# Hybrid decoder trunk on one core: ScalarE evacuation of latents, token-major reciprocals, earlier weight splits and piecewise recurrence units in the first stage

## The chip, the cores and the metric

The kernel runs on one core of a Trainium2 chip. Five engines work side by side, each through its own instructions in order: PE (TensorE, matmul; its weight loads are shown as PEld), DVE (VectorE), ACT (ScalarE), POOL (GpSimd) and SP (SyncE, whose queue issues the DMAs of this stage). The metric is the device time of one execution in microseconds. Each kernel is run several times and the median is compared.

## The reference

Input `x` has 2048 tokens of 1024 numbers. What the first stage computes is the first norm and everything per token that hangs on the input projection; the rest is named in a line each.

```python
h = rmsnorm(x, mix_norm_g)
cols = h @ w_in                      # 35 column chunks of 128 and less: recurrence, gates, q, kv, kr
# recurrence, per head of 64: z = z_in + (prev - z_in) * mu; r, k, v, decay, a, g out of z, then
#   state = state * w + sa * (kk * a) + v * k        over the tokens
# latents, q_d of 384 and kv_d of 256 columns:
q  = rmsnorm(q_d, g_qa) @ w_q_up
kv = rmsnorm(kv_d, g_kva) @ w_kv_up
gate = sigmoid(cols of the gates)
# later stages: causal attention, the scan over chunks, merge and output projection,
# hierarchical mixture of experts, final norm
```

A norm is `y * rsqrt(mean(y*y) + eps) * g`. Here the norm of `x` is not applied to `h` before the projection but to the projected columns, so each chunk is multiplied by the reciprocal root `xrs` of its tokens when it leaves PSUM.

## The kernel before

`phase_a` is the first stage, 0 to 1062 us of the profile. It takes two halves of 1024 tokens, each as `n` = 0, 1 of 512 tokens, with channels on the partitions and tokens along the free side. For each of the 35 chunks of a half (order `worder`: 0 and 1 inputs of the loras, 2 to 13 recurrence, five gates 14 to 18, KV 33 and 34, Q 30 to 32, gate 19, `kr`, the other gates) and each `n`, `a_mm` issues 24 matmuls of 128x512 (three products of a hi/lo split, L151 to L153 in `mm3`) into a PSUM tile of tag `am`, of which there are four. All other small matmuls go through four tiles of tag `rw`.

Weights come by DMA to `awr`; `a_split` (L424) makes hi and lo `aw0`, `aw1` with ScalarE and VectorE or GpSimd, two buffers each, one chunk ahead. A recurrence chunk is evacuated by `a_lerp` (L451: `zin` on VectorE, `zmu` on ScalarE, `z` on VectorE). When three chunks (r, k, v) of a head pair stand, `rw_unit` (L463) prepares the scan: it yields nine times and so has ten pieces. Its names: `kraw`, `ta`, `f`, `bk`, `ar`, `u` are [128 x 512] operands; `aa` are masked products (matmuls L551, evacuation L554); L567 a sum over heads, whose result goes to `bon`; `lora("g")` follows; then three times four transposes (L590) of `hat`, `hat` and `z` go to `rw`, ScalarE copies each to `tok` (L592), and four DMAs from it go to `BKd` (twice) or `Vd`. All of its tiles have one buffer except `hat`; a copy to `tok` waits for the DMAs of the last one. There are eight units in each half, p = 0 to 3 of n = 0, 1. For p < 3 the unit is issued whole, right behind its third chunk; for p = 3 it goes on the list `gens`, and `bg(k)` runs k pieces of that list in between other work, here beside the gates.

KV and Q chunks are latents: `mla_evac` (L253) multiplies by `xrs` on VectorE into `zc` (L259) and squares on ScalarE into `zacc`. `mla_norm` (L273) sums these squares over partitions with a matmul of ones (`sums`, L210), takes root (ScalarE) and reciprocal (VectorE) of the whole [128 x 512] tile and scales. `x_rms` (L228) does the same for `x`. `invert` (L777) is an inversion of small triangular matrices on VectorE (L799, L801), 62 steps that start when the units of a half are stored: it loads `inv` and `si` by DMA, L784 and L792 scale them; then it goes on beside the chunks of KV, Q and gates.

What a function issues is set in order for each engine by a list scheduler when the kernel is built, out of modelled costs; on the chip each engine then goes through its own row in that order. The order of the rows after the edit is therefore shown below, and not only the diff.

Of the kernel before, what the change touches and what calls it, by code (L numbers as in the profile page):

```python
# [10 lines left out]
F32 = mybir.dt.float32  # L11
F32R = mybir.dt.float32r
# [3 lines left out]
AF = mybir.ActivationFunctionType  # L16
OP = mybir.AluOpType
# [4 lines left out]
S, D = 2048, 1024  # L22
# [24 lines left out]
CST = {}  # L47
CFIRST = 128

# [38 lines left out]
class K:  # L88
# [67 lines left out]
    def rope_tables(self, pool):  # L156

        nc = self.nc
        sh = [128, 256]
        self.ropeT = self.dram("ropeT", [2, 8, 16, S])  # L160
        pi = pool.tile(sh, I32, name="posi")
        self.dma(pi, self.I["pos"])
        a, n, z, s, c, u = (pool.tile(sh, F32, name="rt_" + k) for k in "anzscu")
        nc.gpsimd.tensor_copy(u, pi)
# [44 lines left out]

    def sums(self, acc, n, scale):  # L210

        nc = self.nc
        ps = self.pst("rw", 4)
        nc.tensor.matmul(ps, self.c["ones"], acc, start=True, stop=True)
        nc.scalar.activation(n, ps, AF.Sqrt, scale=scale, bias=self.eps[:, 0:1])
        nc.vector.reciprocal(n, n)

# [9 lines left out]

    def x_rms(self, n):  # L228
        self.rs[n] = self.ap.tile([128, 512], F32, name="xrs%d" % n)
        self.sums(self.xacc[n], self.rs[n], 1.0 / D)  # L230

# [21 lines left out]
    def mla_evac(self, pool, ps, key, n, j):  # L253
        nc = self.nc
        if j == 0:
            self.zc[key, n] = (pool.tile([128, 3, 512], F32, name="zc", bufs=2),
                               pool.tile([128, 512], F32, name="zacc", bufs=2))
        zc, acc = self.zc[key, n]
        nc.vector.tensor_tensor(out=zc[:, j], in0=ps, in1=self.rs[n], op=OP.mult)  # L259
        sq = pool.tile([128, 512], F32, name="zsq") if j else acc  # L260
        nc.scalar.activation(sq, zc[:, j], AF.Square)
        if j:
            nc.vector.tensor_tensor(out=acc, in0=acc, in1=sq, op=OP.add)
# [9 lines left out]
    def mla_norm(self, pool, key, n):  # L273
        nc = self.nc
        zc, acc = self.zc.pop((key, n))
        nk, g0, dim = (3, 50, 384) if key == "q" else (2, 53, 256)
        yield "w"
        yield "w"
        rt = pool.tile([128, 512], F32, name="zrs")
        self.sums(acc, rt, 1.0 / dim)  # L280
        cT = [pool.tile([128, 3, 512], F32R, name="cT%d" % j, bufs=2) for j in range(2)]
# [142 lines left out]
    def a_split(self):  # L424
        rv = self.wraw.pop(0)
        hl = [self.ap.tile([128, 8, 128], F32R, name="aw%d" % j, bufs=2) for j in range(2)]
        if rv.shape[2] == 64:
# [7 lines left out]
    def a_mm(self, ci, n, last):  # L435
        while len(self.live) < 2 and self.wraw:
            self.a_split()
# [25 lines left out]
    def rw_unit(self, pool, p, q, zr, zk, zv, x1, xg):  # L463
# [117 lines left out]
        for j, src in enumerate(("b", "k", "v")):  # L581
# [7 lines left out]
            for i in range(4):  # L589
                nc.tensor.transpose(ps[:, i * 128:(i + 1) * 128], x[:, i * 128:(i + 1) * 128], self.ident)  # L590
            tk = t("tok")
            A.activation(tk, ps, AF.Copy)  # L592
# [7 lines left out]
    def phase_a(self):  # L600
# [3 lines left out]
        with ExitStack() as st:  # L604
# [6 lines left out]
            self.wpos = self.wsplit = 0  # L611
            self.wraw, self.live, self.ht, self.zc, self.rs, self.cT, self.xacc = [], [], [[None] * 8, [None] * 8], {}, {}, {}, {}
            gens = []
# [46 lines left out]
            xs = [self.x_load(xp, 0, 0, True)]  # L660
            self.dma(self.c["ones"], self.I["cst"][:, :CFIRST])
            xs.append(self.x_load(xp, 0, 1))
# [6 lines left out]
            for half in range(2):  # L669
                with pool("rw%d" % half) as rp:  # L670
# [26 lines left out]
                    for ci in range(2, 14):  # L697
                        for n in range(2):
# [3 lines left out]
                            if e == 2:  # L702
                                g = self.rw_unit(rp, p, 2 * half + n, z[n, 0], z[n, 1], z[n, 2], x1[n], xg[n])
                                if p == 3:
                                    gens.append(g)
                                else:
                                    for _ in g:
                                        pass
                    for ci in G[:5]:
# [1102 lines left out]
```

## Time and profile before

| | us |
|---|---|
| median of 3 runs | 2710.06 (2707.57 to 2715.52) |
| profiled execution | 2706.18 |
| its span on the core | 2704.4 |
| first stage of it | 0 to 1062 |
| PE busy in the span | 2493.0 (92%) |
| VectorE busy | 1957.0 (72%) |
| ScalarE busy | 1424.3 (53%) |
| GpSimd busy | 961.8 (36%) |

The span is what the profiler saw on the core. The times in all rows below are microseconds from its start. Engines are busy beside one another; a share of busy time says nothing by itself about which of them sets the end.

### The profile page before, as it was taken

The numbers are of one execution on the slowest core, as the hardware profiler recorded it, in microseconds if no ns is written. First come the engines' busy times: TensorE is split into PE (matmuls) and PEld (weight loads), VectorE is DVE, ScalarE is ACT, GpSimd is POOL, SyncE is SP. The second block draws the span as 40 slices with busy tenths as digits, with TensorE's granted clock in tenths as the row PEclk, the third lists the DMA queues.
The fourth block names the chain that finished last, engine by engine and source line by source line (L and its number), as shares of the span: only waits on it lengthen the run. The fifth ranks groups of instructions, "written<-read, shape, count | busy, mean of one in ns | idle before, by whom it ended". The sixth has DMA issues, their size and how long they took to land. (4 is left out here: it accounts for less than half of the span.)

```text
span 2704.4 us, 42459 instructions
## 1 busy us (share of the span) xinstructions
PE 2493.0 (92%) x14868; PEld 2033.2 (75%) x14868; DVE 1957.0 (72%) x3466; ACT 1424.3 (53%) x2539; POOL 961.8 (36%) x676
## 2 busy tenths in 40 slices
PE   8999999999999998989999999999999878999991
PEld 6777778788787886767777777777888667989880
DVE  8766699777748994676666766666666678888883
ACT  6554243465443423666776767632232246878774
POOL 3111612401112222556665665402012145555540
PEclk9999999999999998999999999999999979999995
DMA  4556444435563435444443441674554377999987
GB/s 147 125 146 172 137 140 134 171 102 133 142 177 105 138 122 173 129 122 133 129 123 95 129 129 41 205 225 137 184 167 148 125 228 235 329 288 318 299 246 264
DMA packets 334443, 452.46 MB, mean 167 GB/s; under 512 B 170320, under 2 KB 216272, under 8 KB 332944
## 3 DMA queue, kind: packets, MB, share of 16 engines
q1 hardware_dynamic: 320656, 416.03, 49.3%
q0 software_dynamic: 13568, 33.67, 5.5%
q8 instruction: 118, 1.93, 0.3%
q14 instruction: 101, 0.83, 0.1%
HBM read 318.06 MB, written 138.33 MB: 169 GB/s over the span
## 5 line engine op out<-in xcount | busy, mean ns | idle before, releaser
L151 PE MATMUL am<-h,aw 128*128 128x512 f32 x1104 | 440.8, 400 | 21.2 <-ACT h L237 8.5
L144 POOL TENSOR_TENSOR pl<-pf,ph 128x512 fp32r<-128x512 f32 (+1 forms) x320 | 372.8, 1181 | 238.5 <-ACT ph L143 163.3
L153 PE MATMUL am<-h,aw 128*128 128x512 f32 x1104 | 437.8, 397 | 11.9 <-POOL aw L144 7.5
L152 PE MATMUL am<-h,aw 128*128 128x512 f32 x1104 | 437.3, 396 | 0.1
L1562 PE MATMUL gg<-hh,gu 128*128 128x256 f32 (+5 forms) x1024 | 271.0, 338 | 5.4 <-DVE hh L144 5.0
L151 PEld LDWEIGHTS am<-h,aw 128*128 128x128 f32 x1104 | 210.8, 191 | 70.1 <-ACT h L237 8.5
L153 PEld LDWEIGHTS am<-h,aw 128*128 128x128 f32 x1104 | 210.3, 191 | 60.3 <-POOL aw L144 8.7
L1563 PE MATMUL gg<-hh,gu 128*128 128x128 f32 (+5 forms) x1024 | 249.2, 250 | 0.0
L152 PEld LDWEIGHTS am<-h,aw 128*128 128x128 f32 x1104 | 210.5, 191 | 48.6 <-DVE h L238 2.4
L1052 ACT ACTIVATE pf<-st 128x512 f32<-128x512 f32 (+1 forms) x320 | 167.6, 529 | 119.2 <-PE st L1046 65.2
L1562 PEld LDWEIGHTS gg<-hh,gu 128*128 128x128 f32 x1024 | 195.8, 191 | 13.1 <-DVE hh L144 6.6
L1563 PEld LDWEIGHTS gg<-hh,gu 128*128 128x128 f32 x1024 | 198.6, 194 | 4.5
L143 ACT ACTIVATE ph<-pf 128x512 fp32r<-128x512 f32 (+1 forms) x320 | 176.8, 565 | 6.6
L985 DVE TENSOR_REDUCE mx<-sh 128x1 f32<-128x512 f32 x192 | 128.2, 686 | 66.1 <-PE sh L982 64.9
L144 POOL TENSOR_TENSOR aw<-awr,aw 128x1024 fp32r<-128x1024 f32 (+1 forms) x32 | 89.0, 2782 | 241.2 <-ACT aw L143 231.0
L144 DVE TENSOR_TENSOR gu<-graw,gu 128x1024 fp32r<-128x1024 f32 x128 | 155.0, 1239 | 12.0 <-ACT gu L143 10.3
L143 ACT ACTIVATE gu<-graw 128x1024 fp32r<-128x1024 f32 x128 | 131.1, 1056 | 33.8 <-DMA graw<-in_moe_w_gu 31.4
L801 DVE TENSOR_TENSOR inv<-inv,invt 128x62 f32<-128x62 f32 (+30 forms) x124 | 137.9, 1112 | 2.8
L144 POOL TENSOR_TENSOR sum<-sq,sum 128x512 fp32r<-128x512 f32 x16 | 23.5, 1469 | 317.1 <-ACT sum L143 301.3
L799 DVE TENSOR_TENSOR invt<-inv 128x62 f32<-128x62 f32 (+30 forms) x124 | 133.5, 1076 | 2.6
L1044 PE MATMUL st<-aq,ak 97*128 97x512 f32 (+1 forms) x320 | 127.5, 398 | 8.0 <-ACT pf L1052 7.1
L1580 POOL DMA_INDIRECT x2d<-yo,ix x50 | 93.0, 1860 | 104.2 <-DMA x2d<-yo,ix 21.5
(414 smaller groups left out, 6342.8 us busy)
## 6 DMA issues: line engine op xcount, KB each, us to landing
graw<-in_moe_w_gu SPq DMA_DIRECT2D x128, 512.0 KB
awr<-in_w_cols SPq DMA_DIRECT2D x70, 512.0 KB
draw<-in_moe_w_down SPq DMA_DIRECT2D x62, 512.0 KB
gate<-gsb SPq DMA_DIRECT2D x64, 256.0 KB
SC<-SCd SPq DMA_DIRECT2D x32, 512.0 KB
wbr<-in_w_b SPq DMA_DIRECT2D x32, 512.0 KB
gt<-gate SPq DMA_DIRECT2D x32, 512.0 KB
xs<-in_xT SPq DMA_DIRECT2D x32, 256.0 KB
```

The costliest lines, as they stand in the source:

```text
L143: nc.scalar.activation(hi, src, AF.Copy)
L144: (eng or nc.vector).tensor_tensor(out=lo, in0=src, in1=hi.bitcast(F32), op=OP.subtract)
L151: nc.tensor.matmul(ps, lh, rh, start=first and i == 0, stop=False)
L152: nc.tensor.matmul(ps, lh, rl, start=False, stop=False)
L153: nc.tensor.matmul(ps, ll, rh, start=False, stop=last and i == n - 1)
L799: V.tensor_tensor(out=tv, in0=m[:, 0:t, t:t + 1].to_broadcast([128, t, n]), in1=m[:, t:t + 1, t + 1:].to_broadcast([128, t, n]), op=OP.mult)
L801: V.tensor_tensor(out=m[:, 0:t, t + 1:], in0=m[:, 0:t, t + 1:], in1=tv, op=OP.add)
L985: V.reduce_max(mx[:, j, kb:kb + 1], ps[:, :n], axis=AX)
L1044: T.matmul(ps[:, cs], kk[0][:, ks], qq[0][:, cs], start=True, stop=False)
L1052: A.activation(pf[:, cs], ps[:, cs], AF.Exp, scale=SCALE)
L1562: T.matmul(*a, start=k == 0, stop=False)
L1563: T.matmul(*b, start=False, stop=k == 7)
```

## The change

- The sums of squares come out with tokens on the partitions: four matmuls with the blocks of `acc` as stationary operand and one column of ones give [128 x 4]. Root and reciprocal are taken of that; `spread` copies the result over 128 columns on VectorE and brings it back to [128 x 512] by four matmuls with the identity. For `x` ScalarE copies it on to `xrs`, for the latents it stays in PSUM.
- Latents leave their bank unscaled, by a ScalarE copy; the norm of `x` enters through its column `rc` in `mla_norm`.
- `aw0` and `aw1` have three buffers, and `a_mm` splits until three chunks live.
- `tok` in the units takes the buffer of `f` (tag `f`).
- All units go to `gens`; four pieces are run after each (chunk, n) of 2 to 13.
- The identity comes with the first load of constants, and the tables of the rotary part share two tiles `r1`.

```diff
-CFIRST = 128
+CFIRST = 256
...
-        a, n, z, s, c, u = (pool.tile(sh, F32, name="rt_" + k) for k in "anzscu")
+        a, s = (pool.tile(sh, F32, name="rt_" + k) for k in "as")
+        n, z, c, u = (t[:, o:o + 256] for t in [pool.tile([128, 512], F32, name="r1", bufs=2) for _ in range(2)]
+                      for o in (0, 256))
...
-    def sums(self, acc, n, scale):
+    def sums(self, acc):
         ps = self.pst("rw", 4)
-        nc.tensor.matmul(ps, self.c["ones"], acc, start=True, stop=True)
-        nc.scalar.activation(n, ps, AF.Sqrt, scale=scale, bias=self.eps[:, 0:1])
-        nc.vector.reciprocal(n, n)
+        for i in range(4):
+            self.nc.tensor.matmul(ps[:, i:i + 1], acc[:, i * 128:(i + 1) * 128], self.c["ones"][:, 0:1],
+                                  start=True, stop=True)
+        return ps[:, :4]
+
+    def spread(self, col):
+        b = self.ap.tile([128, 512], F32, name="xacc", bufs=2).rearrange("p (i c) -> p i c", i=4)
+        self.nc.vector.tensor_copy(b, col[:, :, None].to_broadcast([128, 4, 128]))
+        ps = self.pst("rw", 4)
+        for i in range(4):
+            self.nc.tensor.matmul(ps[:, i * 128:(i + 1) * 128], b[:, i], self.ident, start=True, stop=True)
+        return ps
...
     def x_rms(self, n):
         self.rs[n] = self.ap.tile([128, 512], F32, name="xrs%d" % n)
-        self.sums(self.xacc[n], self.rs[n], 1.0 / D)
+        rc = self.rc[n] = self.ap.tile([128, 4], F32, name="xrc%d" % n)
+        nc.scalar.activation(rc, self.sums(self.xacc[n]), AF.Sqrt, scale=1.0 / D, bias=self.eps[:, 0:1])
+        nc.vector.reciprocal(rc, rc)
+        nc.scalar.activation(self.rs[n], self.spread(rc), AF.Copy)
...
-        nc.vector.tensor_tensor(out=zc[:, j], in0=ps, in1=self.rs[n], op=OP.mult)
+        nc.scalar.activation(zc[:, j], ps, AF.Copy)
...
-        rt = pool.tile([128, 512], F32, name="zrs")
-        self.sums(acc, rt, 1.0 / dim)
+        rt, rc, sums = pool.tile([128, 4], F32, name="zrt", bufs=2), self.rc[n], self.sums(acc)
+        for x in (sums, rt):
+            nc.vector.tensor_tensor(out=rt, in0=x, in1=rc, op=OP.mult)
+        nc.scalar.activation(rt, rt, AF.Sqrt, scale=1.0 / dim, bias=self.eps[:, 0:1])
+        nc.vector.reciprocal(rt, rt)
+        nc.vector.tensor_tensor(out=rt, in0=rt, in1=rc, op=OP.mult)
+        rt = self.spread(rt)
...
-        hl = [self.ap.tile([128, 8, 128], F32R, name="aw%d" % j, bufs=2) for j in range(2)]
+        hl = [self.ap.tile([128, 8, 128], F32R, name="aw%d" % j, bufs=3) for j in range(2)]
...
-        while len(self.live) < 2 and self.wraw:
+        while len(self.live) < 3 and self.wraw:
             self.a_split()
...
-            tk = t("tok")
+            tk = t("tok", tag="f")
...
-            self.dma(self.c["ones"], self.I["cst"][:, :CFIRST])
+            self.dma(self.cst[:, :CFIRST], self.I["cst"][:, :CFIRST])
...
                             if e == 2:
-                                g = self.rw_unit(rp, p, 2 * half + n, z[n, 0], z[n, 1], z[n, 2], x1[n], xg[n])
-                                if p == 3:
-                                    gens.append(g)
-                                else:
-                                    for _ in g:
-                                        pass
+                                gens.append(self.rw_unit(rp, p, 2 * half + n, z[n, 0], z[n, 1], z[n, 2], x1[n], xg[n]))
+                            bg(4)
```

The orders below are those of the built kernels; a name ends in the number of its tile, and the brackets hold the engines or DMA queues that the instruction waits for.

ScalarE at the end of half 0's units, before: `tok` copies of the last unit, halves of gates (`gsb`), weights (`aw0`), up-projection weights (`wu0`), squares of latents.

```order
L576 ACTIVATE gw_2515<-rw_2508,pvec_120 128x512 [waits DVE_49]
L592 ACTIVATE tok_2526<-rw_2521 128x512 [waits DMAHW5_49,DMAHW6_49,DMAHW4_49,DMAHW7_49,PE_49,Activation_49]
L634 ACTIVATE gsb_2680<-gsb_2680 128x512 [waits DMAHW3_49,DVE_49,Activation_49]
L592 ACTIVATE tok_2568<-rw_2563 128x512 [waits DMAHW1_49,DMAHW2_49,DMAHW0_49,DMAHW3_49,PE_49,Activation_49]
L143 ACTIVATE aw0_2713<-awr_2589 128x1024 [waits PE_49]
L634 ACTIVATE gsb_2709<-gsb_2709 128x512 [waits DMAHW4_49,DVE_49]
L592 ACTIVATE tok_2579<-rw_2574 128x512 [waits DMAHW6_49,DMAHW5_49,DMAHW7_49,DMAHW0_49,Activation_49]
L634 ACTIVATE gsb_2744<-gsb_2744 128x512 [waits DMAHW4_49,DVE_49]
L143 ACTIVATE aw0_2784<-awr_2653 128x1024 [waits PE_49]
L634 ACTIVATE gsb_2773<-gsb_2773 128x512 [waits DMAHW1_49,DVE_49]
L143 ACTIVATE wu0_3031<-wu_3029 128x256 [waits DMAHW3_49]
L261 ACTIVATE zacc_2816<-zc_2815 128x512 [waits DVE_49]
```

The same place on ScalarE after: `zc` copies out of the KV banks, then the squares.

```order
L597 ACTIVATE gw_2510<-rw_2503,pvec_120 128x512 [waits DVE_49]
L613 ACTIVATE tok_2521<-rw_2516 128x512 [waits PE_49]
L613 ACTIVATE tok_2534<-rw_2529 128x512 [waits DMAHW1_49,DMAHW2_49,DMAHW0_49,DMAHW3_49,PE_49,Activation_49]
L613 ACTIVATE tok_2545<-rw_2540 128x512 [waits DMAHW5_49,DMAHW6_49,DMAHW0_49,DMAHW7_49,PE_49,Activation_49]
L275 ACTIVATE zc_2845<-am_2820 128x512
L275 ACTIVATE zc_2883<-am_2858 128x512
L275 ACTIVATE zc_2845<-am_2904 128x512
L275 ACTIVATE zc_2883<-am_2940 128x512
L277 ACTIVATE zacc_2846<-zc_2845 128x512 [waits Activation_49]
```

The copies of the latents are now ScalarE's and stand right behind the three `tok`; nothing is between.

PE at the first Q matmul of half 0, before: the last KV matmuls (`am_2912`), then Q (`am_2987`).

```order
L152 MATMUL am_2912<-h1_7_1_370,aw0_2784 128x512
L153 MATMUL am_2912<-h0_7_1_369,aw1_2785 128x512
L151 MATMUL am_2987<-h0_0_0_156,aw0_2870 128x512 [waits DVE_49,Activation_49]
L152 MATMUL am_2987<-h1_0_0_157,aw0_2870 128x512
L153 MATMUL am_2987<-h0_0_0_156,aw1_2871 128x512 [waits Pool_49]
```

After: the last unit's transposes (L611, before L590) stand between the last KV matmul (`am_2940`) and Q (`am_3015`).

```order
L152 MATMUL am_2940<-h1_7_1_382,aw0_2743 128x512
L153 MATMUL am_2940<-h0_7_1_381,aw1_2744 128x512
L611 MATMUL rw_2516<-cst_116,hat_2514 128x128 [waits DVE_49]
L611 MATMUL rw_2516<-cst_116,hat_2514 128x128 x3
L611 MATMUL rw_2529<-cst_116,hat_2527 128x128 [waits DVE_49]
L611 MATMUL rw_2529<-cst_116,hat_2527 128x128 x3
L611 MATMUL rw_2540<-cst_116,z2_2263 128x128 [waits DVE_49]
L611 MATMUL rw_2540<-cst_116,z2_2263 128x128 x3
L151 MATMUL am_3015<-h0_0_0_156,aw0_2814 128x512 [waits Activation_49]
L152 MATMUL am_3015<-h1_0_0_157,aw0_2814 128x512
```

The last unit moved down to the KV boundary, and the first Q matmul waits for ScalarE alone where it waited for VectorE and ScalarE.

ScalarE in the middle of half 0's units, before: from one unit's `ta` to `sum0`, with the `tok` of the unit before it.

```order
L506 ACTIVATE ta_855<-rw_852,halfvec_124 128x512 [waits PE_49]
L458 ACTIVATE carry_106<-zmu_1041 128x1 [waits Activation_49]
L592 ACTIVATE tok_786<-rw_781 128x512 [waits DMAHW4_49,DMAHW5_49,DMAHW3_49,DMAHW2_49]
L521 ACTIVATE f_871<-ta_855,halfvec_124 128x512 [waits Activation_49]
L456 ACTIVATE zmu_1080<-carry_106 128x1 [waits DVE_49,Activation_49]
L495 ACTIVATE ex_844<-cum_842 128x8x64 [waits DVE_49]
L497 ACTIVATE en_847<-cum_842 128x512
L534 ACTIVATE ss_883<-rw_880 2x512 [waits PE_49,Activation_49]
L457 ACTIVATE zmu_1080<-zin_1078,pvec_120 128x512 [waits DVE_49]
L592 ACTIVATE tok_797<-rw_792 128x512 [waits DMAHW2_49,DMAHW7_49,DMAHW1_49,DMAHW0_49]
```

After, the same part of a unit (its `ta` stands ahead of the first row):

```order
L516 ACTIVATE ex_913<-cum_911 128x8x64 [waits DVE_49]
L518 ACTIVATE en_916<-cum_911 128x512
L555 ACTIVATE ss_985<-rw_982 2x512 [waits PE_49,Activation_49]
L478 ACTIVATE zmu_1057<-zin_1055,pvec_120 128x512 [waits DVE_49]
L613 ACTIVATE tok_899<-rw_894 128x512 [waits DMAHW2_49,DMAHW3_49,DMAHW1_49,DMAHW0_49]
L479 ACTIVATE carry_106<-zmu_1057 128x1 [waits Activation_49]
L477 ACTIVATE zmu_1143<-carry_106 128x1 [waits DVE_49,Activation_49]
L143 ACTIVATE aw0_1149<-awr_848 128x1024 [waits PE_49]
L478 ACTIVATE zmu_1143<-zin_1141,pvec_120 128x512 [waits DVE_49]
L479 ACTIVATE carry_106<-zmu_1143 128x1 [waits Activation_49]
L542 ACTIVATE f_973<-ta_924,halfvec_124 128x512 [waits DMAHW3_49,DMAHW4_49,DMAHW2_49,DMAHW1_49]
```

The `f` of a unit moved behind the third `tok` of the unit before it and waits for DMA queues, where it waited for ScalarE's own `ta`.

VectorE at the start of half 0's inversion, before.

```order
L784 TENSOR_SCALAR si_2977<-si_2977 128x64 [waits DMAHW2_49]
L785 RECIPROCAL si_2977<-si_2977 128x64 [waits DVE_49]
L259 TENSOR_TENSOR zc_2815<-am_2790,xrs0_325 128x512 [waits PE_49]
L144 TENSOR_TENSOR wu1_3032<-wu_3029,wu0_3031 128x256 [waits DMAHW6_49,DMAHW7_49,DMAHW3_49,Activation_49]
L792 TENSOR_TENSOR inv_2975<-inv_2975,si_2977 128x4096 [waits DMAHW4_49,DMAHW5_49,DMAHW1_49,DMAHW6_49,DMAHW0_49,DMAHW7_49,DVE_49,Pool_49]
L144 TENSOR_TENSOR wu1_3179<-wu_3176,wu0_3178 128x256 [waits DMAHW6_49,Activation_49]
L259 TENSOR_TENSOR zc_2855<-am_2830,xrs1_478 128x512 [waits PE_49]
L799 TENSOR_TENSOR invt_3082<-inv_2975 128x62 [waits DVE_49]
```

After: `zrt` are the four-column operations of the first norm, L816 and L818 the inversion's steps (before L799, L801), L223 the copy of `spread`.

```order
L801 TENSOR_SCALAR si_3005<-si_3005 128x64 [waits DMAHW3_49,DMAHW6_49,DMAHW2_49,DMAHW7_49,DMAHW1_49,DMAHW0_49]
L802 RECIPROCAL si_3005<-si_3005 128x64 [waits DVE_49]
L144 TENSOR_TENSOR wu1_3073<-wu_3070,wu0_3072 128x256 [waits DMAHW0_49,PE_49,Activation_49]
L809 TENSOR_TENSOR inv_3003<-inv_3003,si_3005 128x4096 [waits DMAHW3_49,DMAHW4_49,DMAHW2_49,DMAHW5_49,DMAHW1_49,DMAHW6_49,DVE_49,Pool_49]
L297 TENSOR_TENSOR zrt_3044<-rw_3045,xrc0_326 128x4 [waits PE_49]
L144 TENSOR_TENSOR wu1_3233<-wu_3230,wu0_3232 128x256 [waits DMAHW1_49,Activation_49]
L816 TENSOR_TENSOR invt_3136<-inv_3003 128x62 [waits DVE_49]
L297 TENSOR_TENSOR zrt_3044<-zrt_3044,xrc0_326 128x4 [waits DVE_49]
L818 TENSOR_TENSOR inv_3003<-inv_3003,invt_3136 128x62 [waits DVE_49]
L816 TENSOR_TENSOR invt_3139<-inv_3003 128x122 [waits DVE_49]
L299 RECIPROCAL zrt_3044<-zrt_3044 128x4 [waits Activation_49]
L818 TENSOR_TENSOR inv_3003<-inv_3003,invt_3139 128x61x2 [waits DVE_49]
```

The norm's operations stand behind the inversion's load (L801 waits for DMA queues) and its multiply L809, between its first steps.

## Rows read from the trace of the kernel before

**Rows 1.** The stage table: busy us of PE, its weight loads, VectorE, ScalarE and GpSimd (instructions) in stretches of the first stage, then PE's granted clock, DMA share and GB/s; the last line sums the first stage, 0 to 1062 us.

```profile
295.00:345.00 50.00, 40.95 (x163) 31.43 (x162) 47.07 (x50) 12.26 (x19) 37.04 (x36) 0.94 0.32 100
345.00:545.00 200.00, 192.75 (x860) 158.62 (x859) 178.12 (x188) 79.16 (x132) 59.88 (x29) 0.96 0.45 148
...
820.00:865.00 45.00, 42.03 (x176) 33.55 (x175) 42.92 (x51) 13.30 (x21) 7.61 (x3) 0.96 0.21 69
...
sum 1062.00, PE 1008.24 PEld 817.01 DVE 810.39 ACT 454.37 POOL 242.11; mean PE 126.03 PEld 102.13 DVE 101.30 ACT 56.80 POOL 30.26
```

**Rows 2.** PE's waits in 0 to 1063 us: tile, line, what was waited for, us in total, times, longest us.

```profile
PE rw L567 <- DVE aa L554: 12.9, 8, 2.4
...
PE am L153 <- POOL aw L144: 7.5, 3, 3.7
PE am L151 <- DVE zc L259: 6.0, 2, 3.1
PE rw L214 <- DVE zacc L263: 4.6, 2, 3.1
PE am L153 <- DVE aw L144: 4.4, 3, 3.5
PE am L151 <- ACT aw L143: 4.2, 3, 3.2
```

**Rows 3.** Six short stretches around gaps of PE, columns as in rows 1.

```profile
321.00:329.00 8.00, 4.93 (x13) 3.04 (x12) 7.83 (x10) 3.98 (x6) 7.75 (x9) 0.79 0.21 66
339.00:349.00 10.00, 6.92 (x19) 5.13 (x19) 10.00 (x12) 3.92 (x6) 2.27 (x1) 0.66 0.42 126
489.00:500.00 11.00, 6.94 (x18) 5.21 (x19) 10.76 (x10) 2.58 (x5) 8.44 (x6) 0.69 0.18 47
506.00:513.00 7.00, 4.63 (x15) 3.46 (x14) 5.05 (x6) 3.09 (x5) 5.20 (x5) 0.76 0.36 150
857.00:865.00 8.00, 5.03 (x17) 3.70 (x16) 8.00 (x9) 2.84 (x5) 0.00 (x0) 0.79 0.00 0
1034.00:1049.00 15.00, 8.27 (x23) 5.70 (x21) 8.30 (x5) 4.73 (x7) 6.96 (x3) 0.66 0.38 98
```

**Rows 4.** VectorE's groups of instructions in the first stage: line, operation, tiles, count, then busy us, mean ns of one and idle before.

```profile
L216 DVE RECIPROCAL zrs<-zrs 128x512 f32<-128x512 f32 x8 | 26.7, 3342 | 0.4 <-ACT zrs L215 0.4
...
L216 DVE RECIPROCAL xrs<-xrs 128x512 f32<-128x512 f32 x4 | 13.4, 3347 | 0.7 <-ACT xrs L215 0.6
L259 DVE TENSOR_TENSOR zc<-am,xrs 128x512 f32<-128x512 f32 x20 | 13.2, 673 | 0.0
...
L522 DVE TENSOR_TENSOR f<-z,f 128x512 f32<-128x512 f32 x16 | 11.9, 745 | 1.1 <-ACT f L521 1.0
```

**Rows 5.** PE's timeline: a sum (L214) and the second chunk matmul after it, and one unit's L551. Columns of a timeline: start us, us, engine, line, operation, out<-in, count, and in brackets idle time before it and its releaser.

```profile
28.90 1.02 PE L214 MATMUL rw<-xacc,cst 128*128 128x512 f32 x2
...
30.00 0.40 PE L152 MATMUL rw<-h,aw 128*128 128x512 f32 x1
...
128.15 2.06 PE L551 MATMUL rw<-ar,bk 64*128 64x128 f32 x32
```

**Rows 6.** ScalarE's timeline: the `f` of one unit in the middle of a half, the three `tok` copies of the last unit of half 0, and the third of half 1.

```profile
121.61 0.82 ACT L521 ACTIVATE f<-ta,halfvec 128x512 f32<-128x512 f32 x1
...
266.79 0.59 ACT L592 ACTIVATE tok<-rw 128x512 f32<-128x512 f32 x1
...
277.58 0.60 ACT L592 ACTIVATE tok<-rw 128x512 f32<-128x512 f32 x1 [8.02 <-DMA BKd<-tok]
...
282.51 0.60 ACT L592 ACTIVATE tok<-rw 128x512 f32<-128x512 f32 x1 [2.87 <-DMA BKd<-tok]
...
807.95 0.60 ACT L592 ACTIVATE tok<-rw 128x512 f32<-128x512 f32 x1 [3.02 <-DMA BKd<-tok]
```

**Rows 7.** PE's timeline at the same two units: L567 of each, and eight transposes.

```profile
263.07 0.70 PE L567 MATMUL rw<-sum,blkr 128*128 128x512 f32 x2
...
265.93 1.03 PE L590 MATMUL rw<-cst,hat 128*128 128x128 f32 x8
...
790.91 0.63 PE L567 MATMUL rw<-sum,blkr 128*128 128x512 f32 x2
```

**Rows 8.** SP's queue at the last unit of half 0: the stores of the second and third `tok` (four each) and the load of the inversion.

```profile
278.20 2.56 SPq L96 DMA_DIRECT2D BKd<-tok  x4
...
283.14 2.57 SPq L96 DMA_DIRECT2D Vd<-tok  x4
...
287.34 0.32 SPq L96 DMA_DIRECT2D inv<-Ud  x1
```

**Rows 9.** VectorE's timeline: the four `aa` of a unit in the middle of a half, the start of half 0's inversion, and the first step of half 1's.

```profile
133.32 2.48 DVE L554 TENSOR_TENSOR aa<-rw,cst 128x512 f32<-128x512 f32 x4
...
297.24 0.43 DVE L784 TENSOR_SCALAR si<-si 128x64 f32<-128x64 f32 x1 [11.55 <-DMA si<-ssd]
...
299.15 4.61 DVE L792 TENSOR_TENSOR inv<-inv,si 128x4096 f32<-128x4096 f32 x1
...
828.14 1.94 DVE L799 TENSOR_TENSOR invt<-inv 128x62 f32<-128x62 f32 x1
```

**Rows 10.** ScalarE's waits in 60 to 295 us, columns as in rows 2.

```profile
ACT kraw L509 <- DMA Qd<-bon: 30.4, 7, 5.7
ACT tok L592 <- DMA BKd<-tok: 19.7, 9, 8.0
```

More of the change, by code (lines that the diff above doesn't have):

```diff
@@ L208, in x_load @@
         return xs
-    def sums(self, acc, n, scale):
-        nc = self.nc
+    def sums(self, acc):
         ps = self.pst("rw", 4)
-        nc.tensor.matmul(ps, self.c["ones"], acc, start=True, stop=True)
-        nc.scalar.activation(n, ps, AF.Sqrt, scale=scale, bias=self.eps[:, 0:1])
-        nc.vector.reciprocal(n, n)
+        for i in range(4):
[9 more added lines that the diff above has]
+        return ps
     def x_squares(self, pool, xs, n):
@@ L228, in x_rms @@
     def x_rms(self, n):
+        nc = self.nc
         self.rs[n] = self.ap.tile([128, 512], F32, name="xrs%d" % n)
-        self.sums(self.xacc[n], self.rs[n], 1.0 / D)
+        rc = self.rc[n] = self.ap.tile([128, 4], F32, name="xrc%d" % n)
+        nc.scalar.activation(rc, self.sums(self.xacc[n]), AF.Sqrt, scale=1.0 / D, bias=self.eps[:, 0:1])
+        nc.vector.reciprocal(rc, rc)
+        nc.scalar.activation(self.rs[n], self.spread(rc), AF.Copy)
     def h_make(self, xs, n, k):
@@ L611, in phase_a @@
             self.wpos = self.wsplit = 0
-            self.wraw, self.live, self.ht, self.zc, self.rs, self.cT, self.xacc = [], [], [[None] * 8, [None] * 8], {}, {}, {}, {}
+            self.wraw, self.live, self.ht, self.zc, self.rs, self.rc, self.cT, self.xacc = [], [], [[None] * 8, [None] * 8], {}, {}, {}, {}, {}
             gens = []
```

## The prediction

> **What bounds the kernel now.** I read the stage table first, then TensorE's waits, then the stretches around them. The whole edit lies in the first stage, 0 to 1062 us. There PE is busy 1008.24 of 1062 us, so at most 54 us of its idle time can go, and VectorE, the next engine, is busy 810 [rows 1]. PE paces the stage; what counts is each wait that reaches PE, and each that is added to it. PE's larger waits there are 12.9 us on `aa`, 7.5, 4.4 and 4.2 on the split weights `aw`, 6.0 on a latent that has not left its bank (`zc`), 4.6 on the squares `zacc` [rows 2]. A wait also costs afterwards: six stretches of 7 to 15 us show a granted clock of 0.66 to 0.79, which is PE at 1.2 instead of 2.4 GHz for part of each, always around a gap [rows 3]. Lost clock is window times (1 - clock): 1.7 + 3.4 + 3.4 + 1.7 + 1.7 + 5.1 = 17 us, had PE been busy throughout; with the idle part out, I take 13.
>
> **What goes.** Splitting weights two chunks ahead takes PE's waits on `aw`: 7.5 + 4.4 + 4.2 = 16.1 us. The `zc` and `zacc` waits in their old form go: VectorE no longer carries 20 evacuations of 0.673 us nor twelve 128x512 reciprocals of 3.34 us [rows 4], 53.3 us of VectorE in all (26.7 + 13.4 + 13.2), beside the inversion that fills that engine in 345 to 545 us (178 of 200 us [rows 1]). That is 10.6 us of PE's waits. With the clock that these gaps cost, 13, the removals are worth 16.1 + 10.6 + 13 = 40 us. I take all of it. Nothing of the rest of the 53.3 us is counted, since VectorE's idle time is not what PE waits for otherwise.
>
> **What the sums cost on PE.** One sum was an FP32 matmul of 512 columns: from 28.90 to the matmul at 30.00 lie 1.10 us; one chunk matmul stands between, and these step by 0.23, so 0.87 us is the sum's [rows 5]. Now four with one column, and four of 128 columns to spread. The nearest row is L551, fp32 too, 32 records in 2.06 us, so 16 matmuls at 0.13 us [rows 5]; the dearest reading is 0.87/4 = 0.22 each. A norm then costs 8 x 0.13 - 0.87 = 0.2 us to 8 x 0.22 - 0.87 = 0.9, and 12 of them 2 to 11 us. I take 5. The ScalarE copies that move `xrs` and the four-element operations are hidden where that engine is idle half of the stage (454 of 1062 us busy [rows 1]).
>
> **What the pieces move.** Units 0 to 2 of each `n` no longer run at one go; four pieces follow each chunk. In PE's order the last unit of a half so ends beside the last KV chunk, five matmuls before its end, where it used to end 175 chunk matmuls (40 us) earlier, counted in both orders. Three consequences follow from the orders printed above.
>
> (a) The KV boundary. ScalarE's row holds the three `tok` copies of that unit, and straight behind them the four `zc` copies that free the four `am` banks; the first Q matmul waits for the first of them. The trace gives the pace of the three copies, which share one buffer, each waiting for the DMAs of the one before: in half 0 L567 starts at 263.07 and the third copy ends at 283.11, 20.0 us later; in half 1 790.91 and 808.55, 17.6 us [rows 6, 7]. Between them ScalarE idled 8.02 and 2.87 us for these stores, and PE did not wait for it, since VectorE emptied the gates' banks then. Now PE gets from that point to the first Q matmul in about 4 us (0.7 for the two L567 matmuls, 5 chunk matmuls and three gate-lora matmuls at 0.23, twelve transposes of which eight take 1.03, so 1.5 [rows 7]). The `zc` copy that frees a bank ends 0.7 after the third `tok`, at 18.8 + 0.7. PE stands 15 to 16 us; I take 15 a half.
>
> (b) The first spread. The inversion's load is issued after the last `Vd` store, 4.2 us after the third copy's end (283.11 to 287.34), and its `si` arrives 9.9 us after that (297.24) [rows 6, 8, 9], so about 33 us after L567. VectorE's row has the small operations of the norm behind L801 (before: L784) and L809, the 4.6 us multiply (before: L792 [rows 9]), with some five inversion steps between them (1.94 us for the first [rows 9], less for others). The copy that feeds the spread is done some 43 us after L567; PE, resumed at 19.5, reaches it after 73 chunk matmuls of 0.23 and the sums, at 37. I take 5 us, since inversion steps differ, and 4 for the second spread, which stands behind longer steps of the inversion. Together 9 a half.
>
> (c) The recurrence's own cycle. `tok` and `f` now share one buffer, so the next unit's `f` must wait for the `Vd` stores of the last `tok`: third copy ended (17.6 to 20.0), issue 2.57, landing 1.7 (280.76 to 282.51 between a store's issue and the next copy [rows 6, 8]), so 22 to 24 us after L567. From `f` to the next L567 are `f` 0.82, two products on VectorE at 0.75, L551 2.06 and the four `aa` 2.48, in all 6.9 us [rows 4, 5, 6, 9]. The cycle is 29 to 31 us. PE fills the cycle with the chunk matmuls between two L567, counted in the order of the changed kernel: 101 to 122 in most intervals, which with the unit's own 5.8 us (2.06 of L551 and the loras, transposes and sums) are 29 to 33 us; but one interval of each half has 67, or 21 us. There PE stands 8 to 10, both halves 16 to 20. Against it stands that some of the 12.9 us on `aa` goes when pieces are spread. I take 10, with 0 and 30 as ends.
>
> New gaps also cost clock: each 3 us gap of before is followed by a stretch like 8 us at 0.79, 1.7 us lost [rows 3]. Three such a half are 5, both halves 10.
>
> **Sum.** 2 x (15 + 9) + 10 + 10 + 5 = 73 us added, 40 removed: +33. The profiled execution took 2706.18 us (span 2704.4), the median is 2710.06; from the median I get **2743 us**. A change under 0.3% (8 us) can't be told from none here.
>
> **Rivals.**
> 1. Faster: the boundary's wait doesn't form. ScalarE is only 43% busy in the stage [rows 1], and with no gate stores between the `Vd` and `BKd` stores SP may get the three copies through in some 8 us instead of 18.8; then PE waits 3 to 5 us a half, spreads hide behind the Q chunks, and the sum is -40 + 8 + 5 + 4 = -23, so 2687. For it: VectorE is at 47.07 of 50 us in 295 to 345, 42.92 of 45 in 820 to 865 [rows 1], just where evacuations are moved off it. Against it: the copies' gaps of 8.02 and 2.87 us are releases by DMA, not by ScalarE's load, and the four stores of a copy alone take 2.57 us to issue, so the three can't be nearer than 4.3 us to one another [rows 6, 8]. The Trainium skill, in "Perfetto Trace Analysis", section "Optimizing Scalar/DVE Operations", says that where VectorE is saturated, moving work to ScalarE may make sense; by that rule this rival is the outcome. The rows agree that VectorE is saturated there, and disagree on ScalarE, which has time but stands in a queue behind stores.
> 2. No change: the KV stall forms (30) with its clock (5) and the sums (5), and nothing else: 2710.
> 3. Slower still: the cycle in (c) is longer than PE's in every interval, since ScalarE already waits 30.4 us for `kraw` and 19.7 for `tok` on such stores in 60 to 295 us [rows 10]. At 4 us more in each of 14 intervals that adds 56 less the 10 counted: 2789.
> 4. The edit does less than it says: the list scheduler may order pieces as before. The printed rows exclude it: the `tok` copies do stand before `zc`.
>
> **How the numbers follow.** Forecast 0.57, faster rival 0.16, no change 0.12, slower still 0.15. The forecast's bounds: unknown costs sums 2 to 11, cycle 0 to 30, spreads 0 to 14 a half, removals 27 (waits alone) to 40. These reach from 2710 + 2 x 15 + 2 + 5 - 40 = 2707 to 2710 + 30 + 28 + 30 + 11 + 10 - 27 = 2792. I give 2698 to 2785, which leaves out most of the faster rival and the end of the third. Slower by over 0.3% 0.71, within 0.12, faster 0.17.
>
> **What would show it.** Right: in PE's waits of the changed kernel a first Q matmul L151 of about 15 us in each half on ScalarE, beside three `tok` copies 4 to 10 us apart; L226 waits of 3 to 9 us; `f` on ScalarE released by the `Vd` stores; no PE wait on `aw`. Stretches under full clock at about 300 and 830 us. Wrong: the first Q matmul starts within 5 us of the last KV matmul (rival 1 or 2); L588 waits of several us in nearly every interval (rival 3); waits on `aw` that stay, or a later attention start, since the load of the inversion moves back by some 15 us and the first attention pass needs all that follows it.

## The result, and the profile after

The changed kernel takes 2749.1 us (2736.5 to 2753.79, 4 runs) against 2709.11 us: ratio 1.0143, 95% interval 1.0123 to 1.0163, so 40 us slower. The profiled execution took 2753.79 us with a span of 2751.9. Its first stage ends at 1113.5 us in place of 1061.9; the rest of the span is about 4 us shorter than before. So the whole loss lies in the first stage.

PE's waits there (columns as in [rows 2], to which these answer):

```profile
PE am L151 <- ACT zc L275: 38.7, 4, 14.5
PE rw L572 <- DVE bk L544: 12.6, 4, 6.2
...
PE rw L588 <- DVE aa L575: 5.5, 6, 1.6
PE am L153 <- DVE aw L144: 3.7, 1, 3.7
PE rw L226 <- DVE xacc L223: 3.6, 4, 1.6
```

The waits on split weights shrank from 16.1 to 3.7 us, those on `aa` from 12.9 to 5.5. In their place stand 38.7 us on latents that ScalarE has not yet copied out, and 12.6 us on `bk`, the operand made from `f`. In PE's timeline these are the four `zc` waits and the two long ones on `bk` (the rows from 757.46 on are half 1's). L588, before L567, is the sum over heads of a unit; two rows of it stand around the first `bk` wait and one ahead of the boundary of half 0:

```profile
184.08 0.71 PE L588 MATMUL rw<-sum,blkr 128*128 128x512 f32 x2 [0.93 <-DVE aa L575]
...
210.06 2.26 PE L572 MATMUL rw<-ar,bk 64*128 64x128 f32 x17 [6.20 <-DVE bk L544]
...
214.80 1.19 PE L588 MATMUL rw<-sum,blkr 128*128 128x512 f32 x2 [0.83 <-DVE aa L575]
...
313.09 0.63 PE L588 MATMUL rw<-sum,blkr 128*128 128x512 f32 x2
...
329.73 0.80 PE L151 MATMUL am<-h,aw 128*128 128x512 f32 x1 [12.84 <-ACT zc L275]
...
366.34 0.80 PE L151 MATMUL am<-h,aw 128*128 128x512 f32 x1 [6.99 <-ACT zc L275]
...
757.46 3.88 PE L572 MATMUL rw<-ar,bk 64*128 64x128 f32 x32 [5.95 <-DVE bk L544]
...
876.39 0.79 PE L151 MATMUL am<-h,aw 128*128 128x512 f32 x1 [14.49 <-ACT zc L275]
...
908.68 0.54 PE L151 MATMUL am<-h,aw 128*128 128x512 f32 x1 [4.35 <-ACT zc L275]
```

In half 0 PE passes L588 at 313.09, is through with the unit's transposes at 316.9 and stands 12.84 us; in half 1 it stands 14.49. ScalarE's timeline of half 0 shows why (answering to [rows 6]):

```profile
207.65 0.81 ACT L542 ACTIVATE f<-ta,halfvec 128x512 f32<-128x512 f32 x1 [3.76 <-DMA Vd<-tok]
...
316.92 0.59 ACT L613 ACTIVATE tok<-rw 128x512 f32<-128x512 f32 x1
323.70 0.60 ACT L613 ACTIVATE tok<-rw 128x512 f32<-128x512 f32 x1 [6.20 <-DMA BKd<-tok]
328.59 0.60 ACT L613 ACTIVATE tok<-rw 128x512 f32<-128x512 f32 x1 [4.29 <-DMA BKd<-tok]
329.09 2.06 ACT L275 ACTIVATE zc<-am 128x512 f32<-128x512 f32 x4
...
361.38 1.29 ACT L143 ACTIVATE cT<-zc 128x512 fp32r<-128x512 f32 x2 [7.56 <-DVE zc L304]
...
365.69 1.09 ACT L275 ACTIVATE zc<-am 128x512 f32<-128x512 f32 x2 [0.30 <-DVE cT L144]
```

Three `tok` copies at 316.92, 323.70 and 328.59, the last two released by stores of the one before; then, at once, the four `zc` copies. The third ends 16.1 us after L588 (17.6 to 20.0 in the kernel before). The first row is the other effect: `f` waits 3.76 us for the `Vd` stores of the last unit, and PE, at 210.06, 6.20 us for what comes of it. The second `zc` wait, at 366.34, hangs on the first norm: `cT` waits 7.56 us for VectorE, and the copies of the Q latents stand behind it.

The stage table around both boundaries, and its sum over the stage (columns as in [rows 1]):

```profile
320.00:337.00 17.00, 7.27 (x20) 5.80 (x21) 1.39 (x2) 5.33 (x10) 1.79 (x4) 0.60 0.47 112
...
862.00:885.00 23.00, 8.61 (x27) 6.85 (x28) 1.38 (x2) 5.57 (x11) 0.73 (x1) 0.63 0.60 156
...
sum 1113.00, PE 1032.51 PEld 838.29 DVE 780.25 ACT 471.22 POOL 239.00; mean PE 93.86 PEld 76.21 DVE 70.93 ACT 42.84 POOL 21.73
```

The granted clock falls at each long wait: 0.60 over 17 us and 0.63 over 23 us, where the stretches around the short gaps of before show 0.66 to 0.79 over 7 to 15 us [rows 3].

The first stage was also summed over PE's rows: the time from each PE instruction to the next, split into idle, lost clock (half of the busy time in stretches at 1.2 GHz) and work. The last column is run 1 below; its profiled execution took 2725.22 us, 6 us above that run's median.

| first stage, us | before | changed | changed, own `tok` buffer |
|---|---|---|---|
| ends at | 1061.9 | 1113.5 | 1075.2 |
| PE idle, after the first matmul | 45.3 | 72.2 | 39.5 |
| lost clock | 13.7 | 20.0 | 15.3 |
| sums and spreads of the norms | 7.3 | 20.6 | 20.3 |
| all other PE work | 987.3 | 992.8 | 992.1 |

### The profile page after: what moved, and what is told of

It reads as the page before. It is cut to its first block, busy times and chain, and to the rows that moved or that the text cites. A ratio compares the mean times of both kernels' runs of the same rounds, so it can differ in the third digit from the quotient of the medians.

```text
span 2751.9 us, 42823 instructions
## 1 busy us (share of the span) xinstructions
PE 2518.8 (92%) x15036; PEld 2055.7 (75%) x15036; DVE 1930.6 (70%) x3482; ACT 1441.6 (52%) x2569; POOL 956.8 (35%) x676
## 5 line engine op out<-in xcount | busy, mean ns | idle before, releaser
L151 PE MATMUL am<-h,aw 128*128 128x512 f32 x1104 | 441.4, 400 | 47.0 <-ACT zc L275 38.7
L144 DVE TENSOR_TENSOR gu<-graw,gu 128x1024 fp32r<-128x1024 f32 x128 | 158.0, 1263 | 12.4 <-ACT gu L143 11.6
L143 ACT ACTIVATE gu<-graw 128x1024 fp32r<-128x1024 f32 x128 | 130.9, 1056 | 31.0 <-DMA graw<-in_moe_w_gu 30.7
L818 DVE TENSOR_TENSOR inv<-inv,invt 128x62 f32<-128x62 f32 (+30 forms) x124 | 126.6, 1021 | 2.4
L816 DVE TENSOR_TENSOR invt<-inv 128x62 f32<-128x62 f32 (+30 forms) x124 | 126.1, 1017 | 2.3
```

The lines of the kernel that those rows point to most:

```text
L143: nc.scalar.activation(hi, src, AF.Copy)
L144: (eng or nc.vector).tensor_tensor(out=lo, in0=src, in1=hi.bitcast(F32), op=OP.subtract)
L151: nc.tensor.matmul(ps, lh, rh, start=first and i == 0, stop=False)
L816: V.tensor_tensor(out=tv, in0=m[:, 0:t, t:t + 1].to_broadcast([128, t, n]), in1=m[:, t:t + 1, t + 1:].to_broadcast([128, t, n]), op=OP.mult)
L818: V.tensor_tensor(out=m[:, 0:t, t + 1:], in0=m[:, 0:t, t + 1:], in1=tv, op=OP.add)
```

## The experiments

Ratios are to the kernel before on the same chip. Place names, lines and edits are those of the changed kernel, unless a run starts from the kernel before.

**1. `tok` in a buffer of its own.**

```diff
-            tk = t("tok", tag="f")
+            tk = t("tok", tag="zwa")
```

> The changed kernel, with the three tok copies of a unit in a buffer of their own (that of the lora inputs, idle by then) in place of the buffer of f. Units then stand 75 to 86 chunk matmuls apart in PE's order, as before the change, and the last ends 182 chunk matmuls earlier, far from the KV boundary. Theory (the shared buffer is the cause): PE's waits on zc (38.7 us in the changed kernel) and on bk (12.6) go nearly whole, with some 17 us of lost clock: 2749 - 68 = about 2681 to 2695 us, below the kernel before. Rival (the pieces are the cause, as the prediction had it for the boundary): only the cycle's 12.6 us on bk go, zc waits stay, about 2735.

2719.28 us, ratio 1.0027 (1.0008 to 1.0045): 30 us of the 40 are back. The theory's place holds and its size doesn't (it had 2681 to 2695): `zc` is gone from PE's waits and 0.9 us of `bk` are left, but others have grown.

```profile
PE rw L588 <- DVE aa L575: 13.4, 9, 2.3
PE rw L226 <- DVE xacc L223: 12.2, 4, 7.1
...
PE rw L216 <- DVE zacc L279: 6.5, 2, 4.9
```

The norm's squares and the spread's copy, 6.5 + 12.2 us, now end last at the boundary. Where the units stand in PE's order explains the rest (number of chunk matmuls ahead of the sum over heads of each unit of half 0, counted in the built order):

```
before                     217 303 378 455 534 616 700 780
changed                    218 336 451 557 624 738 842 955
changed, own tok           218 303 378 455 534 616 694 773
changed, whole units       218 336 451 557 624 738 842 955
before, tok shares with f  217 336 451 557 624 741 859 960
```

**2. Units issued whole again**, `tok` still in `f`'s buffer.

```diff
-                                gens.append(self.rw_unit(...))
-                            bg(4)
+                                g = self.rw_unit(...)
+                                if p == 3:
+                                    gens.append(g)
+                                else:
+                                    for _ in g:
+                                        pass
```

> The changed kernel with the units of p below 3 issued whole again, as in the kernel before; tok still in f's buffer. The units stand at the same places in PE's order as in the changed kernel. Theory (shared buffer): no difference, 2741 to 2757 us, zc and bk waits within 5 us of the changed kernel's. Rival (pieces): the boundary wait goes, some 2700.

2750.66 us, 1.0157 (1.012 to 1.0194), with 38.4 us on `zc` and 12.1 on `bk`. The scheduler makes the same order of whole units and of pieces (in both traces the rows of PE, ScalarE and VectorE follow one another alike through the whole stage); the rival falls, and with it the prediction's reason for the boundary.

**3. The shared buffer alone**, in the kernel before.

```diff
-            tk = t("tok")
+            tk = t("tok", tag="f")
```

> The kernel before with one change: tok takes the buffer of f. Units then stand at the same places in PE's order as in the changed kernel (105 chunk matmuls apart, the last at the KV boundary), latents still leave by VectorE. Theory (the shared buffer and where it puts the units is the loss): 25 to 40 us more than the kernel before, 2735 to 2752. Rival (the loss needs ScalarE's copies of the latents behind the tok copies): only the cycle costs, 5 to 15 us more, 2715 to 2727.

2738.86 us, 1.0114 (1.0078 to 1.0149), some 31 us: the theory. The run adds the wait for the buffer and the new places of the units together; no run has one without the other, so their shares are read from the waits alone. With VectorE evacuating, the boundary's wait shows on the next links:

```profile
PE rw L214 <- DVE zacc L263: 19.0, 2, 10.2
PE rw L551 <- DVE bk L523: 9.2, 6, 6.3
PE rw L788 <- DVE si L785: 8.4, 2, 4.4
```

**4. Latents copied out by VectorE.**

```diff
-        nc.scalar.activation(zc[:, j], ps, AF.Copy)
+        nc.vector.tensor_copy(zc[:, j], ps)
```

> The changed kernel with the raw latents copied out of their banks by VectorE in place of ScalarE; all else, the shared buffer too, stays. Theory: the four zc waits go (38.7 us) with about half of the added lost clock, the bk waits stay: 2700 to 2715. Rival (VectorE is full there, with the inversion): the waits come back as VectorE's zc behind the inversion's multiply, 2735 to 2750.

2754.8 us, 1.0149 (1.0101 to 1.0197): no gain, so the theory falls here, and the rival's reason is not the right one either. VectorE was idle and took the copies at once, at 315.57; but the squares are ScalarE's and stand behind the same `tok` copies. VectorE, then ScalarE:

```profile
315.57 2.49 DVE L275 COPY zc<-am 128x512 f32<-128x512 f32 x4 [0.58 <-PE rw L611]
330.36 0.69 DVE L279 TENSOR_TENSOR zacc<-zacc,zsq 128x512 f32<-128x512 f32 x1 [12.30 <-ACT zsq L277]
```

```profile
316.00 0.59 ACT L613 ACTIVATE tok<-rw 128x512 f32<-128x512 f32 x1
323.29 0.60 ACT L613 ACTIVATE tok<-rw 128x512 f32<-128x512 f32 x1 [6.69 <-DMA BKd<-tok]
328.18 0.60 ACT L613 ACTIVATE tok<-rw 128x512 f32<-128x512 f32 x1 [4.29 <-DMA BKd<-tok]
328.67 1.14 ACT L277 ACTIVATE zacc<-zc 128x512 f32<-128x512 f32 x2
```

The last `tok` copy at 328.18, the first square at 328.67, `zacc` at 330.36, and PE, which had gone on with Q, waits 9.03 us there:

```profile
331.11 1.87 PE L216 MATMUL rw<-cst,zacc 128*128 128x1 f32 x8 [9.03 <-DVE zacc L279]
```

Its waits as a sum:

```profile
PE rw L216 <- DVE zacc L279: 17.9, 2, 9.0
...
PE rw L226 <- DVE xacc L223: 12.5, 4, 5.3
...
PE am L151 <- DVE zc L275: 6.7, 4, 5.0
```

These are 37.1 us in the stage for 42.3 (38.7 + 3.6) in the changed kernel. Who empties the banks moves the place of the wait and, within 5 us, not its size.

**5. The same with `tok` in its own buffer** (edits 1 and 4 together).

> The changed kernel with tok in a buffer of its own and the raw latents copied out by VectorE. Against the run with tok alone on ScalarE's copies (2719): Theory (ScalarE's copies help once no tok copies stand ahead of them): 8 to 18 us slower, 2727 to 2737. Rival (who evacuates doesn't matter, the waits are those of the spread): 2713 to 2725.

2718.47 us, 1.0039 (1.0023 to 1.0055), as run 1: the rival. The evacuating engine doesn't matter in either place of the units.

**6. Weights split one chunk ahead**, three buffers kept.

```diff
-        while len(self.live) < 3 and self.wraw:
+        while len(self.live) < 2 and self.wraw:
```

> The changed kernel with weights split one chunk ahead again; three buffers stay, all else stays. Theory (the earlier split is what took the 16.1 us of waits on aw, and 13 us of clock with them): these come back, 2760 to 2780, unless they fall into the new gaps. Rival (these waits went for other reasons, such as less work on VectorE): 2745 to 2753.

2755.36 us, 1.0151 (1.011 to 1.0191), between the ranges of theory and rival. The waits on `aw` stay away (4.2 us left, 3.7 in the changed kernel); the earlier split is not what removed them. The third buffer may be; two buffers in the changed kernel weren't tried.

**7. Third buffer and earlier split alone**, in the kernel before:

```diff
-        hl = [self.ap.tile([128, 8, 128], F32R, name="aw%d" % j, bufs=2) for j in range(2)]
+        hl = [self.ap.tile([128, 8, 128], F32R, name="aw%d" % j, bufs=3) for j in range(2)]
...
-        while len(self.live) < 2 and self.wraw:
+        while len(self.live) < 3 and self.wraw:
...
-            tk = t("tok")
+            tk = t("tok", tag="zwa")
-        rt = pool.tile([128, 512], F32, name="zrs")
+        rt = self.ap.tile([128, 512], F32, name="xacc", bufs=2)
```

(and the rotary tables as in the change).

> The kernel before with three weight buffers and the split two chunks ahead. For space tok lies in the idle buffer of the lora inputs (as alone as before), the latent norm's tile in the idle buffer of x's squares, and the rotary tables share tiles as in the change. Theory: the waits on aw (16.1 us) and their clock (some 8) go, 2685 to 2697. Rival (other waits take their place, the changed kernel with the split one chunk ahead having been no slower): 2704 to 2714.

2707.92 us, 1.0003 (0.9983 to 1.0023): the rival. Of the waits on `aw` 0.2 us are left, and others came, one of them (L1000) behind the stage:

```profile
PE rw L152 <- DVE cT L144: 8.1, 5, 3.6
...
PE rw L1000 <- DVE mr L996: 7.5, 1, 7.5
PE am L151 <- DVE gsb L635: 7.5, 1, 7.5
```

PE ended the stage at 1056.7, 5 us earlier; then it waited 7.5 us on VectorE at the first attention passes (L1000). The latent norm's tile in another buffer may have a part in the waits on `cT`.

**8. Token-major sums alone**, in the kernel before; `sums` has the change's four matmuls, `spread` is the change's, latents still leave scaled.

```diff
-        nc.scalar.activation(n, ps, AF.Sqrt, scale=scale, bias=self.eps[:, 0:1])
-        nc.vector.reciprocal(n, n)
+        self.nc.scalar.activation(rt, ps[:, :4], AF.Sqrt, scale=scale, bias=self.eps[:, 0:1])
+        self.nc.vector.reciprocal(rt, rt)
+        return self.spread(rt)
```

> The kernel before with the token-major sums and spreads alone; latents still leave scaled by VectorE, weights one chunk ahead. PE's sums and spreads took 20.6 us in the changed kernel where the sums before took 7.3. Theory: 13 us of PE's time, less 5 to 10 of the zacc and zc waits since 40 us of reciprocals leave VectorE, plus new waits for the spread's copy of up to 12: 2715 to 2730. Rival (VectorE's relief wins): 2690 to 2705.

2708.57 us, 1.0001 (0.9987 to 1.0014): between theory and rival. PE's idle time in the stage falls from 45.3 to 34.3 us and lost clock from 13.7 to 10.2; on PE the sums' 13 us and 5 us more of its other work take it back.

**9. Whole units, own `tok`** (edits 1 and 2).

> The changed kernel with tok in a buffer of its own and the units of p below 3 issued whole. Against the run with tok alone moved (2719): Theory (pieces or whole make no difference, since the scheduler puts the units at nearly the same places): 2713 to 2725. Rival (what is left over, some 7 to 10 us, is the pieces' cost): 2705 to 2712.

2714.98 us, 1.0017 (1.0004 to 1.0031), in the theory's range. With run 1 at 1.0027 the intervals overlap: whether the pieces cost a few us stays open.

**10. Sums and earlier split together**, in the kernel before (edits 7 and 8, the norm's tile being gone).

> The kernel before with the token-major sums and the third weight buffer with the split two ahead, each of which alone changed nothing; tok alone in its buffer, units whole, latents scaled by VectorE. Theory (the two add: the waits on aw, 10.6 us with the sums alone, go, and the sums cost nothing): 2690 to 2702. Rival (the two collide as in the changed kernel with its own tok buffer, which was 7 to 10 us slower than the kernel before): 2710 to 2722.

2714.23 us, 1.002 (1.0001 to 1.0038): the rival. Two edits that each change nothing don't add to a gain; 12.4 us of waits on the spread's copy stand where run 8 had 10.4 and the weights.

**11. The spread's copy on ScalarE**, added to run 10.

```diff
-        self.nc.vector.tensor_copy(b, col[:, :, None].to_broadcast([128, 4, 128]))
+        self.nc.scalar.activation(b, col[:, :, None].to_broadcast([128, 4, 128]), AF.Copy)
```

> As the run with sums and lookahead, and the copy that feeds each spread is made by ScalarE in place of VectorE. Theory (that copy stands behind the inversion's steps on VectorE, PE waits some 10 us for it): 5 to 10 us less than that run. Rival (the norm's root, reciprocal and squares on VectorE stand behind the same steps, so the wait only moves): within 4 us of that run.

2706.69 us, 0.9991 (0.9976 to 1.0006): 7.5 us less than run 10 as medians, as the theory had it, but the intervals of both runs overlap and the waits on that copy only went from 12.4 to 11.4, so the theory isn't shown. It is no faster than the kernel before that these runs could tell.

**12. Two buffers for `tok`**, in the kernel before.

```diff
-            tk = t("tok")
+            tk = t("tok", bufs=2)
```

> The kernel before with two buffers for tok. The units' copies then wait less for the stores, which is the other direction of the shared buffer. Theory (PE was not held by that wait in the kernel before, its units fit PE's cycle): no change, 2700 to 2714. Rival (shorter cycles help as longer ones hurt): 2685 to 2698.

2707.72 us, 0.9993 (0.998 to 1.0006): the theory. ScalarE's waits on `tok` fell from 19.7 [rows 10] to 9.3 us in 60 to 295 us, and PE gained nothing from it. No run beat the kernel before beyond its interval.

## Why the prediction was right, and where not

The time came within 6 us of the forecast, slower as forecast; single terms of the sum were off by more than that.

- **The KV boundary (a)**, 15 us a half: measured 12.84 and 14.49, at the place and behind the three `tok` copies named. What moved the unit there was wrong: the prediction gave it to the pieces. Run 2 takes these away and changes nothing; run 3 adds only the shared buffer and puts the units there. Step (c) named that buffer, but as a cost of the cycle alone. An engine's row is made by a scheduler that knows the wait too: in half 0 it set the seven intervals of 75 to 86 chunk matmuls between units to 67 to 118, which moves the last unit by 175. That ScalarE evacuates (the "straight behind") isn't needed for the loss, by runs 3 and 4.
- **The spreads (b)**, 18 us over both halves: the waits on the spread's copy came to 3.6 us; VectorE's timeline of half 0 has L801 29.5 us after L588, where 33 were expected, and the copy L223 at 38.4 for 43, so PE hardly waited there; the wait moved on to the second `zc`, 6.99 and 4.35 us, behind that norm. In all 15. The prediction's sign for this term, L226 waits of 3 to 9 us, didn't come: the longest is 1.6.

```profile
342.54 0.20 DVE L801 TENSOR_SCALAR si<-si 128x64 f32<-128x64 f32 x1 [7.73 <-DMA si<-ssd]
...
343.58 4.80 DVE L809 TENSOR_TENSOR inv<-inv,si 128x4096 f32<-128x4096 f32 x1
...
351.54 0.42 DVE L223 COPY xacc<-zrt 128x512 f32<-128x512 f32 x1
```

- **The cycle (c)**, 10 us: the cycle itself was sized right, 30.7 us from L588 to L588 in the short interval of half 0 (184.08 to 214.80), where 29 to 31 were forecast. In it PE stood 6.20 us on `bk` (5.95 in half 1) and 0.83 on `aa`, where 8 to 10 were expected, and its own part took 23.7 us in place of 21, some of it at 1.2 GHz. Over the stage `bk` came to 12.6 us and `aa` fell by 7.4. Net 5.
- **The sums**, 5 us in bounds of 2 to 11: 13.3 measured, beyond the bounds. The row taken (L551, 0.13 us) was too cheap; its matmuls have 64 rows where these have 128, but no run shows that this is the reason. PE's timeline of the first sum of a latent:

```profile
338.72 0.95 PE L216 MATMUL rw<-cst,zacc 128*128 128x1 f32 x8
339.53 0.48 PE L151 MATMUL am<-h,aw 128*128 128x512 f32 x1
```

Eight records of one column took 0.81 us (338.72 to 339.53), so 0.20 for a matmul; the spreads 0.9 for 128 columns. Both are about the dearest reading, 0.22, and the old sum took less than the 0.87 set against them (7.3/12 = 0.61 without idle), which is what puts 12 norms beyond the upper bound.

- **New lost clock**, 10 us, against 13 given back: the stage's lost clock rose from 13.7 to 20.0, so 6 net where -3 was forecast. The new gaps were priced at 1.7 us each, by gaps of 3 us. Four stretches at 1.2 GHz, around the two long `bk` waits and the two boundaries (columns as in [rows 1]):

```profile
205.90:219.50 13.60, 8.61 (x43) 7.41 (x44) 10.97 (x16) 4.28 (x8) 1.46 (x1) 0.50 0.32 79
321.90:335.60 13.70, 5.87 (x14) 4.67 (x15) 1.39 (x2) 5.33 (x10) 0.56 (x2) 0.50 0.42 91
...
755.40:765.60 10.20, 7.29 (x40) 6.38 (x41) 9.68 (x14) 3.16 (x6) 1.46 (x1) 0.50 0.27 74
864.60:881.70 17.10, 5.30 (x13) 4.15 (x14) 1.38 (x2) 5.33 (x10) 0.00 (x0) 0.50 0.49 110
```

Half of PE's busy time in them is lost: 4.3 and 3.6 us at the `bk` waits, 2.9 and 2.7 at the boundaries, whose stretches are mostly idle. The other 6.5 us lie around the second `zc` waits and one wait on `aw`.

- **The removals**, 40 us: the step that failed most. The 16.1 us on `aw` fell to 3.7, but run 7, where 0.2 are left, shows them replaced by others, and run 8 shows the 10.6 us of `zc` and `zacc` replaced by 10.4 on the spread's copy. With the shared buffer out (run 1) the stage's idle time is only 5.8 us under before. In the changed kernel the whole idle time rose by 26.9 where 31 was forecast.

Sum of the stage in the two profiled executions: idle 26.9, clock 6.3, sums 13.3, other PE work 5.5, so 52 us where 33 were forecast. The medians differ by 40 only: 4 us are given back after the stage, and the two profiled executions lie 4.7 us above and 2.9 below their medians. So the nearness of the forecast is partly luck: idle time came out as a whole, with removals and stalls both counted too high, and clock and sums too low.

The rest of run 1, some 7 us above the kernel before, is given back clearly neither by the pieces (run 9) nor by the evacuating engine (run 5); run 10, with neither, stands at 1.002. All of these have the token-major sums, which alone (run 8) changed nothing, since idle time and lost clock fell as well. Summed as in the table, PE's other work is 987.3 to 987.8 us in the four profiles with the old sums (before, runs 3, 7 and 12) and 990.9 to 994.1 in the ten with the new ones. So the new form costs PE some 18 us, 13 in its own matmuls and about 5 in the others, which the prediction put at 5 in all; what makes the other matmuls take longer stays open. The faster rival fell as the prediction argued: ScalarE was busy 471 of 1113 us and yet stood in its queue behind stores. The Trainium skill's page "Perfetto Trace Analysis", section "Optimizing Scalar/DVE Operations", says that where VectorE is saturated, moving some work to ScalarE may make sense. The runs show no gain from it here: 1.0143 with ScalarE evacuating and 1.0149 with VectorE (run 4), and with `tok` in its own buffer 1.0027 and 1.0039 (runs 1 and 5).

## What to carry to other kernels

Sharing a buffer, here to save 2 KB of each partition, is an edit to the order: read, in the built order, where the work that now waits has gone, and what stands behind it on its engine. A wait that is taken away is worth its length only if nothing waits behind it: run 7 took 16 us of waits away and changed the time by nothing. And count what the new form costs the engine that paces the stage: run 8 took 11 us off PE's idle time and gave them back as PE's own work. Test the parts alone before explaining the whole by the most visible one.

## What the runs showed of the hardware that was not expected

An FP32 matmul with one column takes about as long as one with 128 (0.20 and 0.22 us), so a sum over partitions in four pieces of one column costs PE more than one of 512 columns. Longer waits did not lose more clock: around PE's waits of 13 and 14.5 us the stretches at 1.2 GHz were 13.7 and 17.1 us long, but PE was busy in only 5.9 and 5.3 us of them; around its waits of 6 us on `bk` they were 13.6 and 10.2 us long, with PE busy for 8.6 and 7.3.
